# A sixth seven-product unit in the second feed-forward layer, and one DRAM sum fewer per unit in the first

## The chip, the cores and the metric

The kernel runs on one core of a Trainium2 chip. A core has five engines that work at the same time, each through its own queue in order: TensorE (matmuls; PE in the profile, its weight loads PEld), VectorE (DVE), ScalarE (ACT), GpSimd (POOL) and SyncE (SP, which here only issues transfers). Sixteen DMA engines move data for all queues. They wait for each other by semaphores. TensorE writes to PSUM; the other data lie in SBUF, 128 partitions wide. The metric is the device time of one execution in microseconds, the median of several runs.

## The reference

An encoder of two layers over 256 tokens of width 2048, all in float32. The first layer mixes by pooling and attention, the second by a matrix memory; after each mixer stands a gated feed-forward layer, the part that the change touches:

```python
def conv_ffn(x, w_up, conv_w, conv_b, w_down):
    u = x @ w_up                                   # 256 x 2048 by 2048 x 11264
    up = jnp.pad(u, ((0, 0), (1, 1), (0, 0)))
    c = conv_w.astype(u.dtype)
    u = c[0] * up[:, :-2] + c[1] * up[:, 1:-1] + c[2] * up[:, 2:] + conv_b.astype(u.dtype)
    gate, val = jnp.split(u, 2, axis=-1)
    return (jax.nn.silu(gate) * val) @ w_down      # 256 x 5632 by 5632 x 2048
```

Its input is the RMS-normalised x, and its result is added to x.

## The kernel before

**Products in three parts.** TensorE multiplies float32 numbers that are split into a high and a low part. A product of two matrices is high x high, high x low and low x high, summed in PSUM. The activations are split once. Each weight chunk (128 partitions x 1024, 512 KB) is loaded by SyncE, its high part made by a cast on ScalarE (L151) and its low part by a subtraction on VectorE (L152); the two together are the tile `hl`. `Stream` does this some chunks ahead of use: in the feed-forward layers up to seven raw chunks and five split ones are held.

**The feed-forward layer.** The 5632 inner columns are worked in K chunks `FCH` of 4, 8, 8, 8, 8 and 8 tiles of 128. A tile `f` stands for its gate and its value columns. For each tile of K chunk `c` there is an up-projection (`up`, plan step `("n", c, i)`, four weight chunks of 16 matmuls each), then the convolution, the gate and the split of the result (`tail`, L957 to L966) on VectorE and ScalarE into `g`. When the K chunk is complete, four down-projections (`dn`, `("d", c, b)`, one for each 512 columns of the output, four weight chunks of 12 matmuls) add it to x. These quarters of `n` and `d` are the plain slots of the plan; the downs of one K chunk stand between the ups of the next.

**Units of seven products.** Four tiles of a K chunk (half 0 or 1 of it) may instead be computed by a unit, `quads`: the 256 tokens, the pairs of K tiles and the four tiles with their two column blocks are taken as 2 x 2 blocks, and seven block products (with sums of activations, `sx`, and sums of weights) replace eight. A unit passes twice over the eight pairs `p` of K tiles: a first pass with two weight chunks for each pair (four products, `p1`, `p5`, `p6`, `p4`, each three matmuls of 512), a pause of three slots in which results are copied, and a second pass with one chunk for each pair (`p5`, `p6`, on a sum of weight blocks) and one for every two pairs (`p1`): 28 chunks of two products. Then four groups of four transposes (`finish`, L1080) bring the results back into the layout of `tail`. The unit's seven products need four PSUM banks of the pool `ps`, which the transposes share.

**The sums of weights.** Each pair needs sums of its weight blocks. They can be made on the way, by VectorE in the loaded chunk (`sums`, L136 to L142), or in advance in DRAM: SyncE copies blocks into a DRAM tile `G`, and GpSimd issues accumulating transfers into it (`make_step`, up to L128, four parts per pair; parts 0 and 1 are the copies with an accumulation, parts 2 and 3 accumulations within `G`). The last number of a unit in `UNITS` says which: 0, all on VectorE; 1, four sums in DRAM (the whole pair is copied, 1 MB, and a half of it is accumulated); 2, three sums in DRAM (three quarters are copied), and the fourth is added by VectorE in the second pass (kind `left`, L139) before the cast and the split of that chunk.

**What sets the order.** `_ffn_plan` lists the plain slots and sets each unit's 28 steps evenly between two slots: `(c, h, lo, hi, made)` is K chunk, half, first and last slot, kind of sums. The weights stand in the stream in that order, and `places` says at which number of the stream's load each pair's four parts are issued, and how far apart. TensorE's queue is in the order of the plan; `Weave` sets transposes and small products between. VectorE's, ScalarE's and GpSimd's queues are ordered by the framework's scheduler, with some instructions kept in program order.

```python
UNITS = (
    ((2, 1, 18, 57, 1), (3, 1, 64, 90, 1), (4, 1, 97, 141, 0), (5, 1, 148, 174, 1)),
    ((1, 1, 17, 39, 2), (2, 1, 46, 67, 2), (3, 1, 74, 97, 2), (4, 1, 104, 128, 2), (5, 1, 135, 157, 2)),
)
```

Of the kernel before, what the change touches and what calls it, by code (L numbers as in the profile page):

```python
# [219 lines left out]
def trunk(ctx: ExitStack, tc: tile.TileContext, gx, xT, xn, call, catt, cml, weights, make, out):  # L220
# [716 lines left out]
    def ffn_layer(layer, norm, nxt):  # L937
        with ExitStack() as es:
# [203 lines left out]

            wv.add(sums_ready(), 14.0)
            st.la, st.sa, st.more = 7, 3, (lp(f"fw{layer}", 1), lp(f"fh{layer}", 1), st.at + len(_ffn_plan(layer)))
            gts, run, late = {}, {}, set()
            def g_of(c):
# [4 lines left out]
            for step in _ffn_plan(layer):  # L1151
                kind, c = step[:2]
                key = step[:3]
                if key not in run:
                    f0 = sum(FCH[:c])
                    run[key] = (up(f0 + step[2], g_of(c), step[2]) if kind == "n" else
                                down(c, gts[c], step[2]) if kind == "d" else
                                quads([f0 + 4 * step[2] + j for j in range(4)], c, 4 * step[2], f"{layer}_{c}{step[2]}"))
                next(run[key], None)
# [64 lines left out]
def _down_chunks(w):  # L1224
# [6 lines left out]


UNITS = (
    ((2, 1, 18, 57, 1), (3, 1, 64, 90, 1), (4, 1, 97, 141, 0), (5, 1, 148, 174, 1)),
    ((1, 1, 17, 39, 2), (2, 1, 46, 67, 2), (3, 1, 74, 97, 2), (4, 1, 104, 128, 2), (5, 1, 135, 157, 2)),
)


def _ffn_plan(layer):

    slots = []
    for c, n in enumerate(FCH):
        fill = [("n", c, i) for i in range(n) if not any(u[0] == c and u[1] == i // 4 for u in UNITS[layer])]
        if c:
            per = len(fill) // NB
            fill = sum(([*fill[per * b : per * b + per], ("d", c - 1, b)] for b in range(NB)), [])
            if c == 2 and any(u[:2] == (1, 1) for u in UNITS[layer]):
                fill = [fill[i] for i in (0, 2, 1, 4, 3, 6, 5, 7)]
        for e in fill:
            slots += [e] * (4 if e[0] == "n" else FCH[e[1]] // 2)  # L1250
    here = [[] for _ in slots]
    m = KT // 2
    for c, h, lo, hi, _ in UNITS[layer]:
        one, two = 2 * m, m + m // 2
        step = (hi - lo - 3) / (one + two)
        for k in range(one + two):
            here[int(lo + k * step + (3 if k >= one else 0))].append(("s", c, h))
    plan = []
    for e, extra in zip(slots, here):
        plan += [e] + extra  # L1260
    for b in range(NB):
        plan += [("d", len(FCH) - 1, b)] * (FCH[-1] // 2)
    return plan
# [15 lines left out]
def _ffn_order(layer, up, dn, four, last):  # L1279

    pos, seq = {}, []
    m = KT // 2
    d0 = [sum(FCH[:c]) // 2 * NB for c in range(len(FCH))]
    for step in _ffn_plan(layer):
        kind, c, i = step
        n = pos.get(step, 0)
        pos[step] = n + 1
        if kind == "n":
            seq.append(up[(sum(FCH[:c]) + i) * 4 + n])
        elif kind == "d":  # L1290
            seq.append(dn[d0[c] + i * (FCH[c] // 2) + n])
        else:
            u = [e[:2] for e in UNITS[layer]].index((c, i))
            made = UNITS[layer][u][4]
            if n >= 2 * m and (n - 2 * m) % 3 == 2:
                seq.append(last[u, (n - 2 * m) // 3])
                continue
            at = n // 2 if n < 2 * m else (n - 2 * m) // 3 * 2 + (n - 2 * m) % 3
            q, key = four[u, at], f"{layer}{c}{i}_{at}"
            if n >= 2 * m:  # L1300
                seq.append(("made", ((key, 1, 2), q[:, 1024:1536])) if made == 1 else ("left", q[:, 512:1536]))
            elif n % 2:
                seq.append(("made", ((key, 2, 4),)) if made else ("chain", q[:, 1024:2048]))
            else:
                seq.append(("made", (q[:, 0:512], (key, 0, 1))) if made else ("sum", q[:, 0:1024]))
    return seq
# [122 lines left out]
```

## Time and profile before

| what | value |
|---|---|
| median of three runs | 2163.57 us (2163.4 to 2163.76) |
| profiled execution, its time | 2163.53 us |
| its span, first to last instruction | 2161.8 us |
| first feed-forward layer | 256 to 972 us |
| second layer's mixer | 972 to 1450 us |
| second feed-forward layer | 1450 to 2158 us |
| busy: TensorE, VectorE, ScalarE, GpSimd | 2156.9, 1692.5, 1298.0, 237.7 us |

In the rows of groups and stretches, `xN` is a count, the first number after the bar or the stretch is busy time, and the arrow names what ended an engine's idle time. Busy time of matmuls overlaps, since a matmul starts before the one ahead of it has ended; what a matmul costs is the time from its start to the next one's. In names, buffer numbers are left out: `p` is any product of a unit, `w` a raw weight chunk, `hl` a split one, `c` a unit's result. The DMA share of a stretch is the mean busy share of sixteen engines.

### The profile page before, as it was taken

The page shows a single profiled execution, that of the slowest core. Times are in us where ns is not written, and L with a number is a line of the kernel's source. Part 1 is how long each engine was busy: PE and PEld are TensorE (multiplying, and loading weights), DVE is VectorE, ACT ScalarE, POOL GpSimd, SP SyncE. Part 2 cuts the span into 40 slices and gives each one's busy share as a digit, 9 for nine tenths or more (in the row PEclk, how much of TensorE's full clock was granted, in tenths as well). Part 3 has the DMA queues.
Part 4 walks back from the last instruction along what each step waited for, and adds up shares of the span by engine and source line. Part 5 has one row for each costly group of instructions (what it writes and reads, how often), then busy time and mean ns, then how long its engine had stood idle before and what let it go on. Part 6 is the DMA issues. An engine that isn't in the chain of part 4 may idle for free.

```text
span 2161.8 us, 30889 instructions
## 1 busy us (share of the span) xinstructions
PE 2156.9 (100%) x10968; PEld 1832.6 (85%) x10968; DVE 1692.5 (78%) x2367; ACT 1298.0 (60%) x1824; POOL 237.7 (11%) x296
## 2 busy tenths in 40 slices
PE   9999999999999999999999999999999999999999
PEld 7888888888888888889888888888888888888887
DVE  7686698787798787866777676669898878879785
ACT  7665566666565575656554544556676665757663
POOL 0121111110101001101111111110000001000000
PEclk9999999999999999999999999999999999999999
DMA  9878899999989989979888998887999999877773
GB/s 330 246 217 258 257 270 336 337 301 314 319 269 315 299 257 319 314 207 247 257 264 246 260 251 243 271 234 222 312 287 304 303 294 283 279 251 234 261 243 125
DMA packets 189278, 585.66 MB, mean 271 GB/s; under 512 B 23642, under 2 KB 25986, under 8 KB 188354
## 3 DMA queue, kind: packets, MB, share of 16 engines
q1 hardware_dynamic: 157216, 523.03, 69.6%
q0 software_dynamic: 28832, 56.90, 17.3%
q10 hardware_dynamic: 3074, 3.75, 0.8%
q8 instruction: 86, 1.41, 0.3%
q14 instruction: 70, 0.57, 0.1%
HBM read 581.45 MB, written 115.39 MB: 322 GB/s over the span
## 4 chain that ended last, share of the span: by engine, by line
PE 100%; DVE 0%; issue 0%
PE up L267 27%; PE dn L267 22%; PE p L267 16%; PE op L267 8%; PE mv L267 4%; PE mq L267 4%; PE mk L267 4%; PE mo L267 4%; PE qproj L267 3%; PE pool L267 1%; PE kproj L267 1%; PE vproj L267 1%; PE tr L1080 1%; PE av L267 1%; PE qk L267 1%; PE end L267 1%
## 5 line engine op out<-in xcount | busy, mean ns | idle before, releaser
L152 DVE TENSOR_TENSOR hl<-w,hl 128x1024 fp32r<-128x1024 f32 (+1 forms) x880 | 1061.7, 1217 | 335.6 <-ACT hl L151 323.4
L151 ACT CAST hl<-w 128x1024 fp32r<-128x1024 f32 (+1 forms) x879 | 913.6, 1049 | 643.7 <-PE up L267 140.0
L267 PE MATMUL up<-xx,hl 128*128 128x512 f32 (+1 forms) x3328 | 605.5, 337 | 0.0
L267 PEld LDWEIGHTS up<-xx,hl 128*128 128x128 f32 x3328 | 526.3, 188 | 82.6
L267 PE MATMUL dn<-hl,g 128*128 128x512 f32 x2064 | 491.2, 391 | 0.0
L267 PEld LDWEIGHTS dn<-hl,g 128*128 128x128 f32 x2064 | 385.0, 188 | 78.8
L267 PE MATMUL p<-hl,sx 128*128 128x512 f32 x864 | 227.1, 390 | 0.0
L267 PEld LDWEIGHTS p<-hl,sx 128*128 128x128 f32 x864 | 157.5, 188 | 29.8 <-DVE hl L152 0.2
L267 PE MATMUL p<-hl,xx 128*128 128x512 f32 x648 | 174.7, 390 | 0.0
L128 POOL DMA_DIRECT2D G<-G x128 | 119.2, 931 | 345.2 <-DMA G<-in_q 192.9
L124 POOL DMA_DIRECT2D G<-in_q x80 | 64.6, 808 | 673.6 <-DMA G<-in_q 649.7
L267 PEld LDWEIGHTS p<-hl,xx 128*128 128x128 f32 x648 | 117.7, 188 | 21.6
L267 PE MATMUL mk<-xx,hl 128*128 128x512 f32 (+1 forms) x512 | 92.2, 338 | 0.0
L267 PE MATMUL mq<-xx,hl 128*128 128x512 f32 (+1 forms) x512 | 92.2, 337 | 0.0
L267 PE MATMUL mv<-hl,xx 128*128 128x512 f32 (+2 forms) x480 | 91.8, 350 | 0.0
L267 PE MATMUL op<-hl,cat 128*128 128x512 f32 x384 | 91.6, 393 | 0.0
L267 PE MATMUL mo<-hl,xx 128*128 128x512 f32 x384 | 90.5, 391 | 0.0
L267 PE MATMUL op<-hl,mcat 128*128 128x512 f32 x384 | 89.5, 392 | 0.0
L267 PEld LDWEIGHTS mq<-xx,hl 128*128 128x128 f32 x512 | 79.3, 188 | 11.6
L267 PEld LDWEIGHTS mk<-xx,hl 128*128 128x128 f32 x512 | 79.0, 188 | 11.4
L267 PEld LDWEIGHTS mv<-hl,xx 128*128 128x128 f32 x480 | 78.3, 189 | 11.2
L120 POOL DMA_DIRECT2D G<-in_q x48 | 38.1, 793 | 428.1 <-DMA G<-in_q 417.3
(244 smaller groups left out, 1912.4 us busy)
## 6 DMA issues: line engine op xcount, KB each, us to landing
w<-in_up SPq DMA_DIRECT2D x208, 512.0 KB, 5.9
w<-in_dn SPq DMA_DIRECT2D x176, 512.0 KB, 5.5
w<-in_m_in SPq DMA_DIRECT2D x124, 512.0 KB, 5.9
G<-G POOLq DMA_DIRECT2D x128, 256.0 KB, 7.6
w<-G SPq DMA_DIRECT2D x64, 512.0 KB, 5.8
w<-in_q SPq DMA_DIRECT2D x64, 512.0 KB, 5.3
G<-in_q SPq DMA_DIRECT2D x48, 512.0 KB, 7.4
w<-in_a_in SPq DMA_DIRECT2D x46, 512.0 KB, 6.2
```

The source lines that it names most:

```text
L120: pin(add.dma_start(G[r, 0:1024], src[r, 512:1536], accum_op=ALU.add))
L124: pin(add.dma_start(G[r, 0:512], src[r, 512:1024], accum_op=ALU.add))
L128: pin(add.dma_start(G[:, at : at + 512], G[:, of : of + 512], accum_op=ALU.add))
L151: (self.nc.vector.tensor_copy if i + c == 0 else self.nc.scalar.copy)(hl[:, 0, c : c + n], w[:, c : c + n])
L152: self.nc.vector.tensor_sub(hl[:, 1, c : c + n], w[:, c : c + n], hl[:, 0, c : c + n].bitcast(F32))
L267: pe.matmul(out_, lhsT, rhs, start=start, stop=stop, skip_group_check=True)
L1080: pe.transpose(tr[:, j, t * P : t * P + P], src[:, c : c + P], ident)
```

## The change

In the second layer a sixth unit, `(4, 0)`, takes the first half of the fifth K chunk (number 4), whose second half was a unit already; so this K chunk has no plain up-projection left, and the layer has 24 - 4 = 20 plain tiles and 168 plain slots, not 184. The units stand closer: the slots over which each is spread fall from 21 to 24 to 15 to 20. Since the downs of K chunk 4 need both its units, the slots of K chunk 5 are listed in another order (three ups before the first down). In the first layer the three units with sums in DRAM have three of them there, not four. The pairs of the second layer are 48, not 40; they begin 276 loads before the layer, not 240, and stand closer: 13 at a distance of 8 and 24 at 6.75, then 11 at 16 (before: 7 at 11, 21 at 7.6, 12 at 17).

```diff
 UNITS = (
-    ((2, 1, 18, 57, 1), (3, 1, 64, 90, 1), (4, 1, 97, 141, 0), (5, 1, 148, 174, 1)),
-    ((1, 1, 17, 39, 2), (2, 1, 46, 67, 2), (3, 1, 74, 97, 2), (4, 1, 104, 128, 2), (5, 1, 135, 157, 2)),
+    ((2, 1, 18, 57, 2), (3, 1, 64, 90, 2), (4, 1, 97, 141, 0), (5, 1, 148, 174, 2)),
+    ((1, 1, 17, 37, 2), (2, 1, 43, 59, 2), (3, 1, 65, 81, 2), (4, 0, 87, 104, 2), (4, 1, 110, 125, 2),
+     (5, 1, 131, 146, 2)),
 )
...
-            if c == 2 and any(u[:2] == (1, 1) for u in UNITS[layer]):
+            units = [u[:2] for u in UNITS[layer]]
+            if c == 2 and (1, 1) in units:
                 fill = [fill[i] for i in (0, 2, 1, 4, 3, 6, 5, 7)]
+            if c == 5 and (4, 0) in units:
+                fill = [fill[i] for i in (0, 2, 4, 1, 6, 3, 5, 7)]
...
-    places.append([(at - 240 + 11 * k, 5) for k in range(7)] + [(at - 162 + 38 * k // 5, 4) for k in range(21)]
-                  + [(at + 17 * k, 8) for k in range(12)])
+    places.append([(at - 276 + 8 * k, 4) for k in range(13)] + [(at - 168 + 27 * k // 4, 4) for k in range(24)]
+                  + [(at + 16 * k, 8) for k in range(11)])
```

What it does to the order, at three places. First TensorE in the second pass of the last unit of the second layer (`p..._51` are the unit's products, `dn` a plain down slot). Before:

```order
L267 MATMUL dn1_4_1_18459<-hl832_18424,g1_4_16889 128x512 x12
L267 MATMUL p5_1_51_17999<-hl833_18462,sx1_13148 128x512 x3
L267 MATMUL p6_1_51_18011<-hl833_18462,sx1_13148 128x512 x3
L267 MATMUL dn1_4_1_18459<-hl834_18479,g1_4_16889 128x512 x12
L267 MATMUL p1_1_51_17998<-hl835_18490,xx3_8844 128x512 x6
L267 MATMUL p5_1_51_17999<-hl836_18508,sx1_13148 128x512 x3
L267 MATMUL p6_1_51_18011<-hl836_18508,sx1_13148 128x512 x3
L267 MATMUL dn1_4_1_18459<-hl837_18519,g1_4_16889 128x512 x12
```

The same place after the change:

```order
L267 MATMUL dn1_4_1_18792<-hl855_18823,g1_4_17353 128x512 x12
L267 MATMUL p5_1_51_18433<-hl856_18841,sx1_13277 128x512 x3
L267 MATMUL p6_1_51_18446<-hl856_18841,sx1_13277 128x512 x3
L267 MATMUL p5_1_51_18433<-hl857_18853,sx1_13277 128x512 x3
L267 MATMUL p6_1_51_18446<-hl857_18853,sx1_13277 128x512 x3
L267 MATMUL dn1_4_1_18792<-hl858_18864,g1_4_17353 128x512 x12
L267 MATMUL p1_1_51_18432<-hl859_18881,xx3_8955 128x512 x6
L267 MATMUL p5_1_51_18433<-hl860_18893,sx1_13277 128x512 x3
```

A plain slot stands after every second or third product chunk where it stood after every first or second.

Second VectorE's queue in a second pass, at its most uneven place (L139 is the sum of kind `left`, L152 the split; the numbers of `hl` are the order in which TensorE needs them). Before, in the second unit of the second layer:

```order
L152 TENSOR_TENSOR hl673_15490<-w673_15413,hl673_15490 128x1024
L139 TENSOR_TENSOR w674_15428<-w674_15428 128x512
L964 TENSOR_TENSOR y1_15_15453<-y1_15_15453 128x256
L152 TENSOR_TENSOR hl675_15519<-w675_15464,hl675_15519 128x1024
L152 TENSOR_TENSOR hl676_15537<-w676_15475,hl676_15537 128x1024
L152 TENSOR_TENSOR hl674_15508<-w674_15428,hl674_15508 128x1024
```

After, in the last unit:

```order
L139 TENSOR_TENSOR w857_18793<-w857_18793 128x512
L964 TENSOR_TENSOR y1_39_18781<-y1_39_18781 128x256
L152 TENSOR_TENSOR hl859_18881<-w859_18821,hl859_18881 128x1024
L139 TENSOR_TENSOR w860_18839<-w860_18839 128x512
L152 TENSOR_TENSOR hl857_18853<-w857_18793,hl857_18853 128x1024
L152 TENSOR_TENSOR hl858_18864<-w858_18810,hl858_18864 128x1024
```

Before, two later chunks were split ahead of chunk 674; now chunk 859 and a sum for chunk 860 stand ahead of 857, and both and 857 ahead of 858.

Third GpSimd's queue late in the first feed-forward layer (`G05` are pairs of that layer's last unit, `G11` pairs of the second layer). Before:

```order
L120 DMA G051_6_6320<-in_q0 64x1024
L128 DMA G051_6_6320<-G051_6_6320 128x512
L120 DMA G051_7_6587<-in_q0 64x1024
L128 DMA G051_6_6320<-G051_6_6320 128x512
L120 DMA G051_7_6587<-in_q0 64x1024
L128 DMA G051_7_6587<-G051_7_6587 128x512 x2
L124 DMA G111_0_7077<-in_q1 64x512 x2
```

After:

```order
L124 DMA G111_0_6431<-in_q1 64x512
L128 DMA G111_0_6431<-G111_0_6431 128x512
L124 DMA G111_1_6605<-in_q1 64x512
L128 DMA G051_6_6364<-G051_6_6364 128x512
L124 DMA G051_7_6645<-in_q0 64x512
L128 DMA G111_0_6431<-G111_0_6431 128x512
L124 DMA G111_1_6605<-in_q1 64x512
L128 DMA G111_1_6605<-G111_1_6605 128x512
```

The pairs of the two layers, which followed each other, now mix, and the first layer's accumulations in parts 0 and 1 are half as wide (512, not 1024).

## The prediction

> **What bounds the kernel now.** I read the page's busy table and its chain first, then the waits of TensorE, then stretches and rows of the two feed-forward layers.
>
> ```profile
> span 2161.8 us, 30889 instructions
> PE   2156.9 (100%) x10968; PEld 1832.6 (85%) x10968; DVE 1692.5 (78%) x2367; ACT 1298.0 (60%) x1824; POOL 237.7 (11%) x296
> PEclk9999999999999999999999999999999999999999
> PE 100%; DVE 0%; issue 0%
> PE wps L291 <- DVE pad L660: 1.2, 1, 1.2
> ```
>
> TensorE is busy for all but 4.9 us of the span, the chain that ended last is TensorE alone, its clock is never cut, and its only listed wait is 1.2 us before the first product. So the time is the sum of its matmuls, and a change pays in full what it removes there until something makes TensorE wait. The profiled execution took 2163.53 us, 0.04 below the median of 2163.57; its span leaves 1.73 us outside, which I keep. Two things can make TensorE wait: the splits of weights (ScalarE's cast, L151, then VectorE's subtraction, L152) and the loads. These stretches show how close both are (columns: length, busy time and count of each engine, clock, DMA share, GB/s):
>
> ```profile
> 256.00:972.00 716.00, 716.00 (x3622) 607.47 (x3622) 589.45 (x782) 444.59 (x589) 83.58 (x104) 1.00 0.94 296
> 1450.00:2158.00 708.00, 708.00 (x3522) 598.67 (x3520) 594.42 (x780) 445.21 (x577) 39.05 (x48) 1.00 0.82 261
> 1501.20:1514.80 13.60, 13.60 (x70) 11.51 (x69) 13.60 (x18) 10.42 (x13) 0.82 (x1) 1.00 0.92 275
> 1621.40:1738.50 117.10, 117.10 (x571) 98.34 (x570) 102.17 (x135) 77.91 (x100) 11.45 (x14) 1.00 0.93 297
> 1678.90:1714.80 35.90, 35.90 (x174) 30.08 (x173) 31.39 (x39) 21.89 (x25) 3.26 (x4) 1.00 0.92 299
> 640.00:972.00 332.00, 332.00 (x1635) 279.94 (x1634) 264.31 (x344) 201.98 (x267) 36.73 (x46) 1.00 0.91 286
> 320.00:480.00 160.00, 160.00 (x834) 136.55 (x833) 131.46 (x178) 102.95 (x139) 24.21 (x30) 1.00 1.02 328
> ```
>
> The first two are the feed-forward layers: VectorE is busy 82% and 84%, and TensorE's column equals the length everywhere, with VectorE full for 13.6 us (third row) and with the DMA engines full for 160 us (last row). Rows four and five are one unit of the second layer with the gap behind it (87% VectorE), and that unit's second pass (87%).
>
> **The sum on TensorE.** Rows of its timeline in the second layer (start, length, what):
>
> ```profile
> 2022.00 2.88 PE L267 MATMUL dn<-hl,g 128*128 128x512 f32 x12
> 2024.72 0.84 PE L267 MATMUL p<-hl,xx 128*128 128x512 f32 x3
> 2031.59 2.94 PE L267 MATMUL up<-xx,hl 128*128 128x512 f32 x16
> 2034.36 0.85 PE L267 MATMUL p<-hl,sx 128*128 128x512 f32 x3
> 2035.05 0.84 PE L267 MATMUL p<-hl,xx 128*128 128x512 f32 x3
> 2035.73 5.72 PE L267 MATMUL up<-xx,hl 128*128 128x512 f32 x32
> 2041.30 2.89 PE L267 MATMUL dn<-hl,g 128*128 128x512 f32 x12
> 1965.91 0.60 PE L1080 MATMUL tr<-cst,c 128*128 128x128 f32 x4
> 1966.27 5.13 PE L267 MATMUL up<-xx,hl 128*128 128x512 f32 x28
> 1971.23 0.60 PE L1080 MATMUL tr<-cst,c 128*128 128x128 f32 x4
> ```
>
> Lengths overlap, so I go from start to start. Sixteen plain matmuls take 2.77 to 2.79 us (2031.59 to 2034.36; half of 2035.73 to 2041.30). Four plain output tiles are 16 such groups: 44.5 us go. A weight chunk of two products takes 2035.73 - 2034.36 = 1.37 us; the sixth unit has 28: 38.2 us come. Four transposes take 0.36 us, and the 28 matmuls between two such groups take 4.96 us where 28/32 of 5.57 is 4.87, so a group costs 0.45; the unit has four: 1.8 us. The sum is -44.5 + 38.2 + 1.8 = -4.5 us: 2159.0 with no new wait.
>
> **What hides the rest: VectorE.** Groups of the whole run (count, busy, mean ns), and a stretch of a second pass:
>
> ```profile
> L152 DVE TENSOR_TENSOR hl<-w,hl 128x1024 fp32r<-128x1024 f32 (+1 forms) x880 | 1061.7, 1217 | 335.6 <-ACT hl L151 323.4
> L432 DVE TENSOR_TENSOR tb_up<-up,tb_up 128x512 f32<-128x512 f32 x52 | 35.8, 688 | 25.6 <-ACT tb_up L431 25.4
> L139 DVE TENSOR_TENSOR w<-w 128x512 f32<-128x512 f32 x48 | 32.8, 684 | 0.0
> L1082 ACT COPY tb<-tr 128x512 f32<-128x512 f32 x36 | 20.9, 580 | 6.0 <-PE tr L1080 3.3 <-DVE y L964 2.2
> 1705.71 3.49 DVE L152 TENSOR_TENSOR hl<-w,hl 128x1024 fp32r<-128x1024 f32 x3
> 2063.09 3.50 DVE L152 TENSOR_TENSOR hl<-w,hl 128x1024 fp32r<-128x1024 f32 x3 [1.10 <-ACT hl L151]
> 1709.25 0.99 PEld L267 LDWEIGHTS p<-hl,sx 128*128 128x128 f32 x5 [0.23 <-DVE hl L152]
> ```
>
> Back to back a split costs 1.14 us (three in 3.49) and, by the same overlap of 0.08, the smaller ones 0.60. The sixth unit has 28 splits for 16: +13.7 us; eight sums on VectorE (L139): +4.8; four operations on its results at about 0.66: +2.6; four plain tiles' two additions fall away: -4.9. That is +16 us on 594, in a layer that becomes 4.5 us shorter: 87% in the mean. In the first layer the three units get 24 sums, +14 us on 589 of 716: 84%, where the second layer stands now with TensorE full; I cost it at nothing, its cover being the 14% of VectorE that stays idle. If that cover were gone it would be at most those 14 us.
>
> The units of the second layer also stand closer. Per unit and gap the plain slots fall from 28 to about 22. Six slots are 16.5 us of TensorE and about 6 x 1.8 = 10.8 us of VectorE (a split of 1.14, and 0.3 to 1.0 of its tile's other work), so row four becomes 91.4 of 100.6 us: 91%. The second pass loses two of seven down slots: 31.4 - 2.9 of 35.9 - 5.4 us, 93%. Still under full, but what counts is the order. The row at 1709.25 is the one place of the run where a weight load waited for a split, 0.23 us: two product chunks stand next to each other, and VectorE splits two later chunks first (the three splits from 1705.71, the needed one last), 2.3 us of work ahead of it. After the change adjacent product chunks are the rule in a second pass, and in four of the six units one needed split has two later or neighbouring ones and a sum ahead of it: 1.14 + 0.60 + 1.14 = 2.9 us, 0.6 more. Bounds for these four places: nothing (the chunk is the second of two, used 1.37 us later than its neighbour) and 0.6 + 0.23 each, 3.3 in all; a gain is excluded, since TensorE waits nowhere else. I take a little under half, 1.4 us, since the second chunk's later use covers part of it.
>
> Other edits. The transposes of a unit now end one down half-step (6 matmuls) before the next unit, whose fourth bank takes over the last transpose's bank 9 products later: 15 x 0.227 = 3.4 us, against a copy (L1082) of 0.58 us with 6.0 us of waiting over all 36: nothing. The three-slot pause between the passes stays. SyncE issues 76 more transfers and ScalarE casts 12 more chunks, in a layer where it is busy 445 of 708 us: nothing.
>
> **What hides the rest: transfers.**
>
> ```profile
> q1 hardware_dynamic: 157216, 523.03, 69.6%
> q0 software_dynamic: 28832, 56.90, 17.3%
> w<-in_up SPq DMA_DIRECT2D x208, 512.0 KB, 5.9
> q1 hardware_dynamic: 13152, 44.51, 74.0%
> q0 software_dynamic: 3424, 7.87, 27.7%
> w<-in_up SPq DMA_DIRECT2D x31, 512.0 KB, 9.8
> SPq L100 <- DVE hl L152: 295.3, 180, 3.7
> ```
>
> (Whole run; then 320 to 480 us; then SyncE's longest wait from 1500 to 2100 us.) Of the span, q1 takes 2.88 us per MB of all sixteen engines and q0, the accumulations, 6.57. A weight chunk (0.524 MB) is 1.5 us, a pair with three sums (0.786 MB copied, 0.786 accumulated) 7.4, with four (1.05 and 1.05) 9.9. So the first layer saves 24 x 2.5 = 60 us, the new unit adds 8 x 7.4 + 12 x 1.5 = 77: +17 us over the run. It is unevenly placed. From 640 to 972 us six more pairs are made and three become cheaper: +37 us on 0.91 x 332, a share of 1.02. In the second layer a unit and gap takes 50 chunks and 3.1 pairs, 98 us in 100.6: 0.98, from 0.93. The cover for both is the stretch 320 to 480: share 1.02, loads landing in 9.8 us not 5.9, TensorE full. And loads now start when VectorE frees a buffer (the last row). I cost it at nothing; if that cover is gone, it is the third rival.
>
> [...]
>
> **The rivals.**
> 1. *No wait at all:* 2163.53 - 4.5 = 2159.0. For it: nothing waits now, and VectorE reaches 100% for 13.6 us without harm. Against it: the row at 1709.25, already at its edge.
> 2. *The sum-cast-split sequence binds the second passes.* Each sum on VectorE must be cast by ScalarE before its split, and the row at 2063.09 shows VectorE idle 1.10 us for it. With 4 of 8 such waits unfilled a second pass needs 28.5 + 4.4 = 32.9 us of VectorE for 30.5 of TensorE: 2.4 us short, of which the splits kept ready cover part. Half of it in six units: +7, 2166. Against it: plain splits stand between.
> 3. *The queue binds (slower).* In a first pass of a closer unit 22 chunks and 1.4 pairs are 43.4 us of DMA time in 16 x 1.37 + 6 x 2.75 = 38.4 us, in the second pass 17 and 1.1 are 33.6 in 30.5. If accumulations don't yield, loads are 8 us late by a unit's end; splits kept ready hold about 4. Three units are made beside accumulations: 3 x 4 = 12, 2171. It decides from 9 us of waits on. Against it: the stretch 320 to 480.
>
> **The numbers.** The likeliest case is 2163.53 - 4.5 + 1.4 = 2160.4, its own range 2159.3 to 2162.3 by the bounds 0 and 3.3: chance 0.47. Rival 1 has 0.25, rival 2 0.12, rival 3 0.16. A measurement of this kernel can tell about 0.2%, 4.3 us, from no change; the bound for faster is 2159.2, just above rival 1. So faster 0.25, within 0.59, slower 0.16. The range 2158.8 to 2166 holds all but rival 3.
>
> **What would show it.** Right: TensorE's busy time about 2152.5, 72 matmuls fewer, weight loads of p waiting on L152 for one to two us in all, mostly in second passes; VectorE near 608 us of a layer of 704. Rival 2: those waits at 5 us or more, and VectorE full in second passes. Rival 3: waits of L151 on transfers of w, landings over 10 us after 1500. The prediction is wrong if the plain group does not take 2.78 us beside a denser unit, or if waits appear before 640 us, where only the sums moved.

## The result and the profile after

The changed kernel takes 2171.91 us (median of six runs, 2169.93 to 2174.09) beside 2163.60 for the kernel before on the same chip: a ratio of 1.0039 [1.0026, 1.0052]. It is slower by 8.3 us, 11.5 above the forecast of 2160.4. The page of its profiled execution (2174.09 us, the slowest of the six), span, busy times and the engines of the chain that ended last:

```profile
span 2172.3 us, 30964 instructions
PE 2158.1 (99%) x10896; PEld 1826.3 (84%) x10896; DVE 1722.3 (79%) x2408; ACT 1309.7 (60%) x1840; POOL 264.6 (12%) x328
PE 93%; DMA 3%; DVE 2%; ACT 1%; issue 1%; SPq 0%; ACTq 0%; DVEq 0%
```

The 72 matmuls are gone (10896, before 10968), but the chain now goes through transfers, VectorE and ScalarE. What TensorE waited for, in the list of waits (total, times, longest):

```profile
PE tr L1080 <- DVE c L1057: 3.9, 3, 2.8
PE dn L267 <- ACT g L965: 1.8, 1, 1.8
...
PE p L267 <- DVE hl L152: 1.0, 2, 0.8
PE p L267 <- ACT tb L1082: 0.9, 1, 0.9
PE mk L267 <- DVE hl L152: 0.5, 1, 0.5
PE up L267 <- DVE hl L152: 0.5, 1, 0.5
```

None of these stood in the list of before. From the first product of a stage to that of the next (of the last stage, to the end of the last product), the two traces give:

| stage | before | after | difference |
|---|---|---|---|
| first feed-forward layer | 715.59 | 718.88 | +3.3 |
| second layer's mixer | 478.08 | 479.24 | +1.2 |
| second feed-forward layer | 708.39 | 714.17 | +5.8 |

The stretches that answer to these stages (columns as in the prediction):

```profile
256.00:974.90 718.90, 717.23 (x3619) 606.70 (x3618) 601.24 (x804) 442.02 (x588) 106.33 (x132) 1.00 0.96 297
974.90:1454.00 479.10, 478.46 (x2571) 412.17 (x2570) 330.59 (x511) 247.03 (x339) 81.75 (x101) 1.00 0.90 259
1454.00:2168.00 714.00, 707.37 (x3452) 593.83 (x3450) 610.99 (x797) 459.73 (x593) 35.73 (x44) 1.00 0.83 266
```

TensorE is full in neither feed-forward layer any more. In the second one VectorE is busy 611 of 714 us, 86%, and the DMA engines 83%: neither is full on the whole.

**The second layer.** Against the sum of -4.5 us stand 10.3 us of new losses, most of them at the end of a unit. The largest is at 2005 us, behind the unit of K chunk 4's second half. TensorE and then VectorE in the timeline:

```profile
2000.79 1.08 PE L267 MATMUL p<-hl,xx 128*128 128x512 f32 x4
2001.70 3.64 PE L267 MATMUL up<-xx,hl 128*128 128x512 f32 x20
2005.18 0.27 PE L1080 MATMUL tr<-cst,c 128*128 128x128 f32 x1
2008.24 0.90 PE L1080 MATMUL tr<-cst,c 128*128 128x128 f32 x3 [2.79 <-DVE c L1057]
```

```profile
2002.65 0.74 DVE L1056 SCALAR_TENSOR_TENSOR c<-p,re_n,c 128x512 f32<-128x512 f32 x1
2003.31 2.35 DVE L152 TENSOR_TENSOR hl<-w,hl 128x1024 fp32r<-128x1024 f32 x2
2005.58 0.87 DVE L960 SCALAR_TENSOR_TENSOR y<-tb_up,cst,y 128x255 f32<-128x255 f32 x2
2006.37 1.21 DVE L152 TENSOR_TENSOR hl<-w,hl 128x1024 fp32r<-128x1024 f32 x1
2007.50 0.68 DVE L1057 TENSOR_TENSOR c<-c,c 128x512 f32<-128x512 f32 x1
```

The transposes stand in TensorE's queue 3.5 us behind the unit's last product (2001.70 to 2005.18). They need the combination L1057, and VectorE comes to it only after three splits and two operations of a plain tile's tail, 4.1 us after L1056 has ended (2003.39 to 2007.50). The same wait is 1.00 us at 1702 and 0.18 at 1908. Two others at the ends of units, in the timeline of TensorE at 1620 and at 2129 us:

```profile
1618.74 1.52 PE L267 MATMUL p<-hl,sx 128*128 128x512 f32 x6
1621.20 1.66 PE L267 MATMUL p<-hl,xx 128*128 128x512 f32 x6 [0.94 <-ACT tb L1082]
...
2125.69 3.80 PE L267 MATMUL dn<-hl,g 128*128 128x512 f32 x16
2131.31 3.92 PE L267 MATMUL dn<-hl,g 128*128 128x512 f32 x16 [1.82 <-ACT g L965]
```

At 1620 the next unit's fourth bank is that of the last transpose, whose copy (L1082) starts only at 1620.57, 4.5 us after the transpose has ended; start to start this costs TensorE 1.10 us. At 2129 the last downs need the results of the last unit, whose tail is not through: 1.97 us. With 2.95 + 1.00 + 0.18 for the transposes, 0.4 for splits and 1.6 of a slowed clock behind the wait at 2005 (last section) that is 9.2 of the 10.3; the rest are stretches of about 0.1 us, most of them right behind a wait.

**The first layer.** The wait at 750 us goes back to transfers. The chain that ended last, from 712 us (start, length, what):

```profile
712.20 10.66 DMA G<-in_q
...
722.93 14.62 DMA w<-in_dn
...
737.61 13.85 DMA w<-in_up
...
753.87 12.34 DMA w<-in_dn
```

The weight loads of this chain land after 12 to 15 us, in a stretch in which the second layer's first pairs are made beside the last pairs of the first layer. The mixer's 1.2 us are a wait for a split at 1016 us, behind small transfers of the mixer's own (`gd<-gr`, 7.6 us in the chain); `late_places`, below, has it too.

### The profile page after: what moved, and what is told of

It reads as the page before. It is cut to its first block, busy times and chain, and to the rows that moved or that the text cites. A ratio compares the mean times of both kernels' runs of the same rounds, so it can differ in the third digit from the quotient of the medians.

```text
span 2172.3 us, 30964 instructions
## 1 busy us (share of the span) xinstructions
PE 2158.1 (99%) x10896; PEld 1826.3 (84%) x10896; DVE 1722.3 (79%) x2408; ACT 1309.7 (60%) x1840; POOL 264.6 (12%) x328
## 4 chain that ended last, share of the span: by engine, by line
PE 93%; DMA 3%; DVE 2%; ACT 1%; issue 1%; SPq 0%; ACTq 0%; DVEq 0%
PE up L267 23%; PE dn L267 20%; PE p L267 16%; PE op L267 8%; PE mo L267 4%; PE mk L267 4%; PE mv L267 4%; PE mq L267 4%; PE qproj L267 3%; DVE hl L152 1%; DMA w<-in_dn 1%; PE kproj L267 1%; PE pool L267 1%; PE vproj L267 1%; PE tr L1080 1%
## 5 line engine op out<-in xcount | busy, mean ns | idle before, releaser
L152 DVE TENSOR_TENSOR hl<-w,hl 128x1024 fp32r<-128x1024 f32 (+1 forms) x892 | 1073.7, 1217 | 325.6 <-ACT hl L151 309.9
L151 ACT CAST hl<-w 128x1024 fp32r<-128x1024 f32 (+1 forms) x891 | 923.0, 1048 | 640.5 <-DVE w L139 110.0
L267 PE MATMUL up<-xx,hl 128*128 128x512 f32 (+1 forms) x3072 | 559.5, 338 | 0.5 <-DVE hl L152 0.5
L267 PEld LDWEIGHTS up<-xx,hl 128*128 128x128 f32 x3072 | 485.5, 189 | 76.8 <-DVE hl L152 0.9
L267 PE MATMUL p<-hl,sx 128*128 128x512 f32 x960 | 251.7, 391 | 1.1 <-DVE hl L152 1.0
L124 POOL DMA_DIRECT2D G<-in_q x144 | 120.2, 836 | 1002.2 <-DMA G<-in_q 942.1
L267 PEld LDWEIGHTS p<-hl,sx 128*128 128x128 f32 x960 | 175.9, 188 | 37.6 <-DVE hl L152 3.4
L267 PE MATMUL p<-hl,xx 128*128 128x512 f32 x720 | 191.8, 390 | 0.9 <-ACT tb L1082 0.9
L128 POOL DMA_DIRECT2D G<-G x144 | 140.8, 978 | 360.4 <-DMA G<-in_q 117.8
L267 PEld LDWEIGHTS p<-hl,xx 128*128 128x128 f32 x720 | 131.7, 188 | 26.3 <-ACT tb L1082 1.4
L267 PEld LDWEIGHTS op<-hl,mcat 128*128 128x128 f32 x384 | 71.5, 188 | 14.6
```

The source lines that it names most:

```text
L124: pin(add.dma_start(G[r, 0:512], src[r, 512:1024], accum_op=ALU.add))
L128: pin(add.dma_start(G[:, at : at + 512], G[:, of : of + 512], accum_op=ALU.add))
L151: (self.nc.vector.tensor_copy if i + c == 0 else self.nc.scalar.copy)(hl[:, 0, c : c + n], w[:, c : c + n])
L152: self.nc.vector.tensor_sub(hl[:, 1, c : c + n], w[:, c : c + n], hl[:, 0, c : c + n].bitcast(F32))
L267: pe.matmul(out_, lhsT, rhs, start=start, stop=stop, skip_group_check=True)
```

## The experiments

All kernels were timed beside the kernel before on the same chip, whose median was 2163.51 to 2163.58. A stage's length is that of the profiled execution.

**The first layer's sums alone** (`sums0_only`), on the kernel before:

```diff
-    ((2, 1, 18, 57, 1), (3, 1, 64, 90, 1), (4, 1, 97, 141, 0), (5, 1, 148, 174, 1)),
+    ((2, 1, 18, 57, 2), (3, 1, 64, 90, 2), (4, 1, 97, 141, 0), (5, 1, 148, 174, 2)),
```

> The kernel before with one part of the change: three DRAM sums per unit in the first layer, the fourth on VectorE. Units of the second layer and the places of their pairs as before. Theory A (the loss lies in transfers of pairs that start earlier and closer, and in VectorE and ScalarE being late at the ends of the closer units): no loss here, 2163.6 within 1 us, since 24 pairs become cheaper for the DMA engines and TensorE keeps its 715.6 us in the first layer. Theory B (the 24 sums that VectorE gets in the first layer make its splits late; the first layer took 3.3 us more after the change): 2166.9, the first layer at 718.9.

Measured: 2163.70 us, ratio 1.0002 [0.9993, 1.0011], the first layer at 715.59. Theory B falls: 24 more sums on VectorE cost nothing there, as the prediction had it.

**The places of the pairs with it** (`sums0_places`): the edit just shown, and

```diff
-    places.append([(at - 240 + 11 * k, 5) for k in range(7)] + [(at - 162 + 38 * k // 5, 4) for k in range(21)]
-                  + [(at + 17 * k, 8) for k in range(12)])
+    places.append([(at - 276 + 8 * k, 4) for k in range(13)] + [(at - 168 + 27 * k // 4, 4) for k in range(24)]
+                  + [(at + 16 * k, 8) for k in range(11)])
```

> As the kernel with the sums of the first layer alone, and the 40 pairs of the second layer's five units stand at the first 40 of the changed places (from 276 loads ahead of that layer, at distances of 8 and 6.75). Up to the second layer all transfers are now those of the changed kernel; the second layer is that of before. Theory A: the first layer grows by 3.3 and the mixer by 1.2 us, 2168, and the runs scatter by a microsecond or two as the changed kernel's do; TensorE waits at about 750 and 1015 us for chunks that land 11 us or more after their issue. Theory B: the same time as with the sums alone. If only the second layer's closer units matter: 2163.6.

Measured: 2163.92 us, ratio 1.0004 [0.9995, 1.0013], but with single runs up to 2168.01; the profiled execution has 715.59 and 478.06 and no wait. The stretch from 640 us to the end of the first layer, of this kernel and then of the changed one:

```profile
640.00:971.60 331.60, 331.60 (x1632) 279.52 (x1631) 267.82 (x352) 200.13 (x266) 58.94 (x74) 1.00 1.00 314
```

```profile
640.00:971.60 331.60, 329.93 (x1618) 276.44 (x1617) 266.67 (x350) 198.92 (x265) 59.01 (x73) 1.00 1.00 313
```

In both the DMA engines are full (share 1.00; 0.91 with the sums alone), and only one of the two executions waits. So theory A's half on transfers does not hold as expected: full DMA engines cost 0.3 us in the median and up to 4.4 in single executions, not 4.5 each time.

**Later places** (`late_places`), on the changed kernel:

```diff
-    places.append([(at - 276 + 8 * k, 4) for k in range(13)] + [(at - 168 + 27 * k // 4, 4) for k in range(24)]
-                  + [(at + 16 * k, 8) for k in range(11)])
+    places.append([(at - 240 + 8 * k, 4) for k in range(9)] + [(at - 168 + 27 * k // 4, 4) for k in range(24)]
+                  + [(at + 13 * k, 7) for k in range(15)])
```

> The changed kernel, but the pairs of the second layer start 240 loads ahead of it, not 276, so that they no longer mix with the first layer's last pairs; 33 of the 48 lie ahead of the layer and 15 in it, not 37 and 11. Theory A: the waits at 750 us go (about 3 us), those of the mixer may stay; 2168 to 2169, and less scatter. Theory B: 2172, since the sums of the first layer stay. If transfers bind in the second layer: slower than 2172, as four more pairs are made there.

Measured: 2170.74 us, ratio 1.0035 [1.0022, 1.0047]; the share from 640 us on falls to 0.96 and the first layer is back at 715.59, while the second layer keeps its 714.14. The gain of 1.2 us is within the scatter. In the profiles of all nine kernels with these places the first layer takes 715.59; of the eight with the changed ones, three show 0.3 to 3.3 us more.

**Without the fourth sums** (`no_left1`), on the changed kernel:

```diff
-            if kind == "left":
+            if kind == "left" and i < 554:
```

> The changed kernel without the 48 sums on VectorE in the second layer (the fourth sum of a pair is left out there, and the chunk is split unsummed): 29 us less VectorE work in that layer, all transfers and matmuls as they are. Theory A: the waits of the second layer for VectorE (transposes for the combination of results, products for splits) fall from about 8 us to 2 or 3, so 2166 to 2167, and those of the first layer and the mixer stay. If the second layer's loss were transfers or ScalarE's queue: 2171 to 2172.

This kernel leaves the sums out, so only its time counts, not its result. Measured: 2164.30 us, ratio 1.0003 [0.9994, 1.0012]. The second layer takes 708.68, 5.5 less; VectorE is busy 584 us from 1454 to 2160. One wait for L1057 (1.1 us) and that for the last g (2.0, with 1.6 at a slowed clock) are left. So most of the loss in the second layer goes with 29 us of VectorE's work.

**Moving the ends of units.** `finish6` sets the first transposes later, `end_early` the last unit earlier, `combo` does both with the later places, and `combo_sums` has all four sums of the last three units made in DRAM beside that:

```diff
-                            wv.add(finish(c12, c22, fs[2:], gt, i0 + 2, name), 3.0)
+                            wv.add(finish(c12, c22, fs[2:], gt, i0 + 2, name), 6.0 if layer else 3.0)
...
-    (4, 0, 87, 104, 2), (4, 1, 110, 125, 2),
-     (5, 1, 131, 146, 2)),
+    (4, 0, 87, 104, 2), (4, 1, 109, 124, 2),
+     (5, 1, 128, 143, 2)),
```

> The changed kernel with the first transposes of a second-layer unit set 6 us behind the unit's end in the plan, not 3; work and transfers are the same. Theory A (now: TensorE reaches a transpose before VectorE, late with splits and tails, has made the combination): the waits of tr for L1057 go, 3.9 us, and with them the 1 to 2 us in which the granted clock is at half after the long one: 2171.9 - 5 = 2167. Rival C (VectorE is simply short of time and the lateness moves on, to the bank copy L1082 or to the splits of the next unit): 2171 to 2172.

> The changed kernel with the last unit of the second layer set from slots 131-146 to 128-143 (and the one ahead of it by one slot), so that its results come 8 us earlier, ahead of the last downs which need them. Theory A: the wait of dn for the last g (L965) at 2129 us goes, 2.0 us, and up to 1.5 us at half clock behind it: 2169 to 2170. Rival C: the closer gap makes VectorE later in the last unit, new waits of p for splits, 2172 or more.

> Three edits on the changed kernel: transposes at 6 us, the last unit three slots earlier, and the pairs from 240 loads ahead with 15 in the layer. Theory A: the gains add, 5 + 2.5 + 1.2 us: 2163, with waits of 1 to 3 us left in the second layer (bank copy L1082, splits of p) of which the sum on TensorE knows nothing. Rival C: 2169 to 2171.

> The kernel of the three edits, and the last three units of the second layer take all four sums from DRAM: 24 sums, 14 us, less on VectorE; the transfers grow by 24 x 2.5 = 60 us of all sixteen engines. Theory A: half of what leaving out all 48 sums gave beyond the three edits, at most 2 us: 2161. If transfers bind: loads land 11 us and more after issue in the mixer or the second layer, waits of L151 on w, and a time above that of the three edits alone, 2164 or more.

Measured: 2168.48, 2170.21, 2168.07 and 2168.99 us (ratios 1.0027, 1.0032, 1.0022 and 1.0026, each give or take 0.001). Each aimed wait goes, and others come. In `finish6` none is left for L1057, but the bank copy costs 1.1 and 2.1 us and the last downs 2.7. In `end_early` and `combo` the downs don't wait, but the last unit, now four slots behind the one ahead, does. TensorE in `combo`:

```profile
2009.56 0.86 PE L267 MATMUL p<-hl,sx 128*128 128x512 f32 x3
2014.03 1.65 PE L267 MATMUL p<-hl,sx 128*128 128x512 f32 x3 [3.61 <-ACT tb L1082]
```

and the copy in ScalarE's timeline, with what released it:

```profile
2013.39 0.59 ACT L1082 COPY tb<-tr 128x512 f32<-128x512 f32 x1 [0.37 <-DVE y L960]
```

The transpose was done at 2007.2; the copy writes a tile `tb`, of which there are two buffers, and what releases it is the last operation on such a tile in a tail on VectorE (L960). The plain tiles take their `tb_up` from the same two buffers, and the tail that ends here, at 2013.30, is a plain tile's. From this came theory D. `combo_sums` has this wait at the same length and adds 1.6 us for a split: 14 us less on VectorE bring nothing where the queue of tails binds. Up to here rival C (lateness only moves) had the better of it.

**A third buffer** for `tb`, of the plain tiles and the units alike (`tb3`, `finish6_tb3`, `combo_tb3`, on the kernels of these names):

```diff
-            tp = lp(f"ff{layer}", 2)
+            tp, tbp = lp(f"ff{layer}", 2), lp(f"ft{layer}", 2 + layer)
...
-                u = gather(tp, ps, f"up{layer}_{f}")
+                u = gather(tbp, ps, f"up{layer}_{f}")
...
-                    u = tp.tile([P, 2, S], F32, tag="tb", name=f"tb_{layer}_{f}")
+                    u = tbp.tile([P, 2, S], F32, tag="tb", name=f"tb_{layer}_{f}")
```

> The changed kernel with three buffers, not two, for the tile tb into which a unit's transposes are copied (second layer only). Theory D (formed on the runs so far: the copy L1082 that empties the bank of the last transpose must wait until one of two tb buffers has gone through its tail on VectorE, so a closer unit ends in a queue of tails): the wait of p for L1082 at 1620 us goes, 1.1 us, and those of tr for L1057 and of dn for the last g stay: 2170 to 2171. If VectorE's and ScalarE's load alone sets the copy's time: 2172, the wait stays.

> Transposes at 6 us and three tb buffers on the changed kernel. Theory D: with the transposes alone 2168.5 was left, with waits of p for L1082 of 1.1 and 2.1 us; both go, with up to 1 us at half clock: 2164.5 to 2165.5, the wait for the last g stays (1.6 + 1.1 us and its slow stretch). Rival C (lateness only moves on): 2168.

> The kernel of the three edits and three tb buffers. Theory D: its waits of p for L1082, 1.1 + 3.8 + 0.7 us, and the 2 us at half clock behind them go: 2168.1 - 7.5 = 2160.5, at which the sum on TensorE of the prediction (2159.0) plus 0.4 of split waits and the like stands bare, and faster than the kernel before. Rival C: 2165 or more, with waits of p for splits in the last unit.

Measured: 2169.84, 2173.05 and 2166.31 us. In `tb3` the wait at 1620 is gone and the others are there, as theory D said, with a new one of 1.44 us for a split. In `finish6_tb3` the bank waits are gone, but a down waits 3.85 us for the tail of the unit ahead of it (L965): slower by 4.6 us than with two buffers, a miss. `combo_tb3` gains 1.8 us, not 7.5; the bank copy of the last unit still costs 3.1.

**Narrow units in the kernel before** (`narrow5`):

```diff
-    ((1, 1, 17, 39, 2), (2, 1, 46, 67, 2), (3, 1, 74, 97, 2), (4, 1, 104, 128, 2), (5, 1, 135, 157, 2)),
+    ((1, 1, 17, 37, 2), (2, 1, 46, 62, 2), (3, 1, 74, 90, 2), (4, 1, 104, 119, 2), (5, 1, 135, 150, 2)),
```

> The kernel before with its five units of the second layer as narrow as the changed ones (16 to 20 slots, not 21 to 24), started where they were, so that the gaps between them grow to 9 to 16 slots. Work, sums and transfers are those of before. Theory D: narrow units load VectorE more in their second pass (one to two plain slots fewer there), so that transposes wait for L1057 as in the changed kernel, 1 to 4 us in all, while the wide gaps leave no wait for L1082 or the last g: 2165 to 2168. If the sixth unit's gaps alone are the cause: 2163.6.

Measured: 2166.84 us in 11 runs that all lie between 2166.74 and 2167.05, ratio 1.0014 [1.0005, 1.0023]. The second layer takes 3.4 us more at the same work and the same transfers:

```profile
PE tr L1080 <- DVE c L1057: 1.5, 2, 1.3
...
PE p L267 <- DVE hl L152: 0.3, 1, 0.3
```

Narrowness alone makes the waits for L1057 (0.39 and 1.45 us start to start) and for splits (0.2, 0.2 and 0.45). The wide gaps leave none for the bank or g. Theory D held.

**The sums on GpSimd** (`pool_left1`; `pool_shift` and `pool_shift_tb3` with the later places, shifted windows and, in the last, three buffers):

```diff
-                pin(add(l, l, r))
+                pin((self.nc.gpsimd.tensor_add if i >= 554 else add)(l, l, r))
...
-    ((1, 1, 17, 37, 2), (2, 1, 43, 59, 2), (3, 1, 65, 81, 2), (4, 0, 87, 104, 2), (4, 1, 110, 125, 2),
-     (5, 1, 131, 146, 2)),
+    ((1, 1, 17, 36, 2), (2, 1, 42, 58, 2), (3, 1, 64, 80, 2), (4, 0, 86, 102, 2), (4, 1, 108, 123, 2),
+     (5, 1, 129, 144, 2)),
```

> The changed kernel with the 48 sums of the second layer on GpSimd, not VectorE; TensorE's order is word for word that of the changed kernel, and so are the transfers. Theory E (VectorE's amount of work causes the waits): the time of the kernel without these sums, 2164.3, give or take 1 us. Theory F (it was the order that the scheduler found without them): 2170 or more. If GpSimd's sums are slow or hold up VectorE or the accumulations that GpSimd issues: above 2172, with waits of L151 on GpSimd's w.

> The sums on GpSimd, the pairs from 240 loads ahead with 15 in the layer, and the windows of the units shifted so that all gaps are six slots and the last unit ends two slots earlier. Theory E with the end of the layer as a cause of its own: of what the kernel with the sums on GpSimd has left, the wait of dn for the last g (2.0 us and 1 to 1.6 us at half clock) goes: 2161. Theory F: 2166 or more, with the lateness at another unit's end.

> As the last, and three tb buffers in the second layer. Theory E: no wait for the bank copy L1082 is left, 2160 to 2161, the bare sum on TensorE; if tb is not short any more with GpSimd's help: the same time as without the third buffer.

Measured: 2169.31, 2173.37 and 2174.14 us. These runs did not separate theory E from F as meant, since the move takes little work off VectorE: from 1454 to 2160 us it is busy 607 us in `pool_left1`, not 584 as without the sums. GpSimd's and VectorE's groups in `pool_left1`, then VectorE's in `no_left1` (second layer; count, busy, mean ns):

```profile
L139 POOL TENSOR_TENSOR w<-w 128x512 f32<-128x512 f32 x48 | 77.8, 1682 | 245.0 <-DMA w<-in_q 233.4 <-DVE hl L152 10.7 <-issue 0.8
L152 DVE TENSOR_TENSOR hl<-w,hl 128x1024 fp32r<-128x1024 f32 x331 | 418.3, 1282 | 75.9 <-ACT hl L151 67.6 <-DMA w<-in_q 3.6
```

```profile
L152 DVE TENSOR_TENSOR hl<-w,hl 128x1024 fp32r<-128x1024 f32 x331 | 401.4, 1222 | 88.4 <-ACT hl L151 81.5
```

The two waits of `no_left1` at the ends of units are in `pool_left1` as well (1.1 us for L1057, 2.0 for the last g); beside them it has 3.3 us of waits for splits. In the two shifted kernels no wait is left at the ends of units, but splits held up by the sums cost up to 3.1 us each in the first three units (last section).

**Shifted windows, sums on VectorE** (`shift6`: later places, the windows just shown, transposes at 6 us; `shift6_tb3` with the third buffer; `shift45_tb3` with transposes at 4.5 us):

> The changed kernel with pairs from 240 loads ahead, shifted windows (all gaps six slots, the last unit ending at slot 144) and transposes at 6 us, sums on VectorE. Theory D (waits come from the ends of units and can be placed away): the waits for L1057 and for the last g are gone, those for the bank copy are 1 to 3 us: 2163 to 2165. Theory C (VectorE is short of time, lateness moves): 2167 or more.

> The same with three tb buffers in the second layer. Theory D: no bank wait either; 0.4 and 1.4 us of waits for splits in the first two units are left: 2161 to 2163, at or below the kernel before. Theory C: 2166 or more.

> The same with transposes at 4.5 us. Theory D: as with 6 us, give or take 1 us, since both lie behind the combination and ahead of the bank's next use. Theory C: several us off, up or down, as another order puts the lateness elsewhere.

| kernel | median, us | ratio to before | second layer, us |
|---|---|---|---|
| `shift6` | 2162.51 | 0.9996 [0.9987, 1.0005] | 707.00 |
| `shift6_tb3` | 2160.90 | 0.9988 [0.9979, 0.9997] | 705.35 |
| `shift45_tb3` | 2160.97 | 0.9988 [0.9978, 0.9997] | 705.41 |

The page and the waits of `shift6_tb3`:

```profile
span 2159.2 us, 30951 instructions
PE 2152.7 (100%) x10896; PEld 1826.3 (85%) x10896; DVE 1722.2 (80%) x2408; ACT 1309.3 (61%) x1840; POOL 264.8 (12%) x328
...
PE p L267 <- DVE hl L152: 1.2, 1, 1.2
```

VectorE has the work of the changed kernel (1722.2 and 1722.3 us), TensorE the same matmuls, and the waits at the ends of units are gone: theory D holds, C falls. `combo` and `shift6` differ in the windows alone (six slots, not four, ahead of the last unit, and the others a slot earlier); that is 5.6 us. `shift6_tb3` is 11.0 us faster than the changed kernel and 2.6 faster than the kernel before, and its runs (2160.71 to 2162.17) scatter no more than those.

## Why the prediction was wrong

**The sum on TensorE was right.** In `shift6_tb3`, the changed kernel's work without its waits at the ends of units, the second layer is 708.39 - 705.35 = 3.0 us shorter; with the 1.36 us start to start of the one wait left, and 0.1 behind it, that makes the 4.5 of the sum. TensorE's busy time is 2152.7, forecast about 2152.5; VectorE's in the layer is 610 of 706, forecast 608 of 704. The price of 1.4 us for late splits (bounds 0 and 3.3) was not what failed: in the changed kernel weight loads of the second layer waited 1.8 us for splits, of which TensorE lost 0.4; in `shift6_tb3` it lost 1.36.

**The step that failed is "Other edits ... nothing".** It named the bank of the last transpose and set 3.4 us of room against a copy of 0.58 us; but the copy starts only when a `tb` buffer is free, which waits for tails on VectorE (at 1620 us until 1619.7, and a cast in ScalarE's queue took the 0.9 us behind it). It cost 1.10 us there, up to 3.8 in an experiment. And it priced neither end of that chain at all: the transposes wait for the combination L1057 (4.1 us, and 1.6 at a slowed clock), the last downs for the last unit's g (2.0). The prediction had said "what counts is the order" and then looked for the order's effect at the splits alone. In its own terms, closer units were costed by VectorE's load (91 to 93%, "still under full"); `narrow5` shows that the same load over the layer, only closer, costs 3.3 us.

**"Transfers: nothing" was right in the median of one test and wrong in single executions.** In the first layer the share came to 1.00 (estimate 1.02). The cover, the stretch 320 to 480, does not hold each time: with the same transfers one execution waits 4.5 us ahead of the second layer and another not at all. Why the changed kernel's median lies 2.2 us below its profiled execution, while `sums0_places` lies only 0.3 above before, is not settled; part of the scatter is the slowed clock below, whose mean over a run was 0.998 to 1.000 in the six.

**The rivals.** Rival 3 named 2171, near what was measured, but by a mechanism that is not there: in the second layer from 1500 to 2100 us weight loads land after 5.0 to 5.8 us, and L151 waits on sums, not on transfers. That accumulations don't yield, on which its 12 us rest, was an assumption that no run shows. Transfers were late in the first layer, where its sign ("landings over 10 us after 1500") does not look; that it came near the number was luck. Rival 2 lacked its sign too: the weight loads of p waited 3.4 us for splits in the whole run, not 5 or more in the second passes. Rival 1, no wait at all, is what placement brings within reach: 2160.9 is 1.9 above it. No rival had the ends of units.

## What to carry to other kernels

Where one engine is full, an edit that packs work closer is not priced by the other engines' loads: take the last product of each packed piece and follow what needs its result (the next instruction on the full engine, the bank, the buffer of the copy that empties it, the consumer at the layer's end), with the queue that stands ahead of each link. Such waits move when a single link is moved, and go when all links get their room at once: three edits together left 9.1 us above the bare sum of 2159.0, with the windows 3.5 were left, with the third buffer 1.9. A transfer system at a share of 1.00 must be read from several executions: with the same transfers up to the second layer, one profile here showed 4.5 us lost, another none.

## What the runs showed of the hardware

**A wait of TensorE can cost more than its length.** The stretches behind the waits at 2005 and 2129 us of the changed kernel, then that behind the same last wait without the sums (the column ahead of the DMA share is the granted clock):

```profile
2008.00:2011.00 3.00, 2.76 (x9) 2.45 (x10) 2.88 (x6) 1.79 (x4) 0.00 (x0) 0.50 0.96 356
2131.00:2134.00 3.00, 2.69 (x12) 2.17 (x13) 0.43 (x1) 1.26 (x2) 0.00 (x0) 1.00 0.49 175
```

```profile
2119.80:2125.00 5.20, 5.13 (x15) 4.00 (x16) 1.65 (x2) 1.06 (x2) 0.00 (x0) 0.67 0.33 105
```

At a granted clock of 0.50 matmuls of 512 take 427 ns from start to start, not 227. Of the 23 waits of 1.5 us and more in these profiles (close ones counted as one) 15 were followed by such a stretch; none of the shorter waits that stood alone was. Half speed lasted 3.41 us twelve times, which cost 1.6 to 1.9 us, and 6.83 us three times, which cost 2.3 to 2.9. The same wait of 1.97 us had it in three kernels and not in two, so it also makes runs scatter.

What differs is where the wait falls. Within a profile the changes of the clock lie on one grid of 3.41 us (in that of the changed kernel at 4.36, 2007.99, 2011.40 and 2171.83 us, which are 587, 1 and 47 steps apart), and the grid lies differently in each (in that of the kernel before at 5.98 and 2163.20, 632 steps apart). The two steps of it around the wait at 2129 us in the changed kernel, then the step with the same wait without the sums, and the step behind it:

```profile
2127.45:2130.86 3.41, 2.04 (x10) 1.34 (x8) 2.85 (x5) 1.38 (x3) 0.00 (x0) 1.00 0.65 214
2130.86:2134.28 3.42, 2.97 (x13) 2.41 (x14) 0.62 (x2) 1.45 (x2) 0.00 (x0) 1.00 0.43 153
```

```profile
2117.89:2121.30 3.41, 1.59 (x7) 1.14 (x7) 1.91 (x3) 0.61 (x2) 0.00 (x0) 1.00 0.74 243
2121.30:2124.71 3.41, 3.41 (x9) 2.65 (x9) 1.22 (x1) 1.04 (x1) 0.00 (x0) 0.50 0.09 37
```

In the first the grid cuts the wait, so that TensorE is idle for 1.37 us of one step; in the second all of it, 1.82 us, falls into one. The step ahead of half speed at 2008 us in the changed kernel (2004.58 to 2007.99) has 2.54 us. From 250 to 2150 us of all twenty profiles, half speed began behind each step at full clock with 1.81 us or more of idle time, 15 in all, and behind none with 1.78 or less.

**Beside sums on GpSimd a split took longer.** In `pool_shift`, GpSimd and then VectorE ahead of a wait of 3.09 us of TensorE at 1672 us:

```profile
1664.26 0.79 POOL L124 DMA_DIRECT2D G<-in_q  x1 [8.24 <-DMA G<-in_q]
1664.81 1.56 POOL L139 TENSOR_TENSOR w<-w 128x512 f32<-128x512 f32 x1
1666.05 1.10 POOL L128 DMA_DIRECT2D G<-G  x1
1666.62 4.30 POOL L139 TENSOR_TENSOR w<-w 128x512 f32<-128x512 f32 x3
```

```profile
1661.97 1.21 DVE L152 TENSOR_TENSOR hl<-w,hl 128x1024 fp32r<-128x1024 f32 x1
1667.49 5.66 DVE L152 TENSOR_TENSOR hl<-w,hl 128x1024 fp32r<-128x1024 f32 x2 [4.30 <-ACT hl L151]
```

Two splits that take 2.35 us elsewhere take 5.66 beside three sums: the first takes 4.53 us and ends 1.1 us behind the last sum, the second its usual 1.21. What slows it there, no run shows. The sums are also late themselves: that of 1664.81 stands in GpSimd's queue behind an issue (L124) that waited 8.24 us for a transfer, and the chain to TensorE's wait goes through both.
